# A hybrid encoder layer: zero-padded query remainders, alternating banks for the value transposes, and stores of the intra products from another queue

## The chip, the core and the metric

The kernel runs on one core of a Trainium2 chip. A core has a matrix engine (PE, which loads its stationary operand in a separate step, PEld), a vector engine (DVE), a scalar engine (ACT), GpSimd (POOL) and SyncE (SP, which here only issues DMAs). PE writes its results to PSUM, where DVE and ACT fetch them; operands lie in SBUF. The metric is the device time of one execution in microseconds (us).

## The reference

One encoder layer on 512 positions of 1024 features, in fp32:

```
x = x + 1/2 * SwiGLU_1(RMSNorm(x))
h = RMSNorm(x); p = h @ W_in
  group A: bidirectional gated delta rule, 4 heads of 128, chunks of 64:
      lmat  = strict lower part of (k*beta) k^T * decay,  tmat = (I + lmat)^-1
      intra = q k^T * decay
      scan over chunks: v_new = u - w S;  o = qg S + intra v_new;  S = S*exp(g) + kdec^T v_new
  group B: dilated softmax attention, 8 heads of 64 (queries and keys normalised, relative bias)
x = x + concat(A, B) @ W_out
x = x + 1/2 * SwiGLU_2(RMSNorm(x))
x = RMSNorm(x)
```

## The kernel before

Features lie in partitions and positions in the free dimension, 512 to a tile. An fp32 product is made of parts: a factor is split into a high part, rounded to the PE's fp32r format, and the remainder (names that end in h and l), and a projection sums three matmuls, high by high, high by low and low by high. The first feed-forward block (FFN1) runs until about 383 us, the mixer until about 760 us, the second block (FFN2) until the end.

The mixer's projections are units of a string `ORDER`: K, Q, V and Z are 128 columns each of the delta rule's keys, queries, values and gates, by head; Pa, Pb and v are the attention's queries, keys and values, by pair of heads; g0 to g3 start the grams of the four heads. PE's instruction order is fixed by hand: `interleave` merges the projections with the chain of the delta rule (grams, triangular solve, levels, scan) and with the attention, and each PE instruction is issued after the one ahead of it. The order on ACT, DVE, POOL and SP is made by a scheduler, from dependencies and from the order in which the code names them.

What the change touches:

- The weights of the mixer (`wsp`, L216) were split earlier and lie in DRAM. SP loads a half of a projection's weights at a time, 512 KB, into one of 4 buffers, so each unit needs two. A load can be issued when its buffer is free and SP has come to it.
- `gram(h)` multiplies keys by keys (`pkk`) and keys by queries (`pkq`). For both directions DVE masks `pkq` into `itr`, POOL multiplies it by the decay in `M`, and DVE writes the strict part of `pkk`, scaled, over the same `M`. Then SP stores 8 pieces of `M` to `D1` in DRAM (D in the trace) and the two `itr` to `int_d`; each of these is 128 x 4 runs of 512 bytes. The solve reads `D1` back (`MM`), the scan reads `int_d`.
- `post_val(h)` and `post_v(pr)` transpose the values of one delta-rule head and of one pair of attention heads on PE (`ptr`, `ptv`), and ACT (with DVE for `ptv`) fetches them as `vtok` and `vb`. Both took their PSUM bank from the pool `pat`, which has one bank. `pov` is another pool of one bank, in which `mix` sums the attention's outputs; `pat` also holds the transposed probabilities `pT`.
- `split_pair` prepares one pair of heads for the scores. For head i, `QA[i]` holds the high part of its queries twice, in both halves of the partitions, and `KA[i]` the high part of its keys in one half and their remainder in the other, so one matmul over 128 partitions sums two products. `ql` holds the remainders of the queries, the first head's in partitions 0 to 63 and the second's in 64 to 127.
- `score(n)`, for n from 0 to 31, makes a tile of 128 x 512 scores `pS` with two matmuls, QA by KA over 128 partitions and ql by the high half of KA over 64. DVE adds the bias and takes the maximum (L1070), ACT takes the exponential; `flip` transposes it (`pT`) and splits it (`PT`, ACT and DVE), and `mix` multiplies it by `vb`. The scores of the first half run among the scan's matmuls (`ps`), the last 16 among those of the output projection (`pd`) and of the remaining `pqk`.

Of the kernel before, what the change touches and what calls it, by code (L numbers as in the profile page):

```python
# [10 lines left out]
F32 = mybir.dt.float32  # L11
F32R = mybir.dt.float32r
# [4 lines left out]
P = 128  # L17
T = 512
NKT = 8
NF = 22  # L20
NH = 4
# [69 lines left out]
def encoder_layer(ctx, tc, xT, gu1, dn1, win, wab, wo1, wo2, gu2, dn2, cols, relb, masks, onehot, lnc, sel, out):  # L91
    nc = tc.nc
    te, ve, se, gp, sy = PEQueue(tc, nc.tensor), nc.vector, nc.scalar, nc.gpsimd, nc.sync
# [12 lines left out]
    def pfl(name):  # L106
        return ps.tile([P, T], F32, tag="fl", name=name, bufs=2)

    def pat(name):
        return ps.tile([P, T], F32, tag="at", name=name, bufs=1)  # L110
# [4 lines left out]
    def prg(name):  # L115
        return ps.tile([P, T], F32, tag="rg", name=name, bufs=2)
# [7 lines left out]
    def tmp(tag, name, n=T, dt=F32, bufs=2):  # L124
        return tp.tile([P, n], dt, tag=tag, name=name, bufs=bufs)

    def slot(tag, name=None, dt=F32):
        return xp_.tile([P, T], dt, tag=tag, name=name or tag)
# [31 lines left out]
    def lx(*a, **k):  # L160
        with tc.issue_after(act["pre"].ins):
            return se.activation(*a, **k)
# [58 lines left out]
    def sub(o, a, b):  # L221
        ve.tensor_tensor(out=o, in0=a, in1=b.bitcast(F32), op=ALU.subtract)
# [140 lines left out]
    with ExitStack() as mctx:  # L363
        mp = mctx.enter_context(tc.tile_pool(name="mp", bufs=1, reuse_waits="tile"))

        def mt(shape, name, tag=None, dt=F32, bufs=1):
            return mp.tile(shape, dt, name=name, tag=tag or name, bufs=bufs)
# [77 lines left out]
        def dhc(t):  # L445
            return t.rearrange("p (d h c) -> p d h c", d=2, h=NH)

        vb = {}

        posts = []  # L450

        def proj_v(pr):
            pt = pmm("pvb")
# [4 lines left out]
            yield ("set", f"post{len(posts) - 1}", VGV)  # L458

        def post_v(pr, u):  # L460
            ptv = pat("ptv")
            for c in range(NC):
                te.transpose(out=ptv[:, c * P:(c + 1) * P], in_=u[:, c * P:(c + 1) * P], identity=ident)
            for hh in range(2):
                t = slot(f"x{2 * pr + hh}", "vb", F32R).rearrange("p (j e) -> p j e", j=4)
                src = ptv.rearrange("p (j e) -> p j e", j=4)[:, :, hh * 64:(hh + 1) * 64]
                se.copy(t[:, :, 0:64], src)
                sub(t[:, :, 64:128], src, t[:, :, 0:64])
                vb[2 * pr + hh] = t
# [66 lines left out]
        def sc(t, d, h, c, base=0):  # L536
            i = base + d * 16 + h * 4 + c
            return t[:, i:i + 1]
# [36 lines left out]
        int_d = dr.tile([NC, P, 8, P], F32, name="int_d")  # L575
# [13 lines left out]
        def gram(h):  # L589
            hc = slice(h * 4, h * 4 + 4)  # L590
            pts = []
            for t, new in ((kT, pat), (qT, pov)):
                pt = new("ptk")
                for c in range(NC):
                    te.transpose(out=pt[:, c * P:(c + 1) * P], in_=t[:, h, c * P:(c + 1) * P], identity=ident)
                pts.append(pt)
            yield 0.86, 0.0
            for pt, w in zip(pts, (wk, wq)):
                sq = tmp("sq", "sq2")
                for c in range(NC):  # L600
                    s_ = slice(c * P, (c + 1) * P)
                    se.activation(sq[:, s_], pt[:, s_], AF.Square, accum_out=w[:, h * 4 + c:h * 4 + c + 1])
            se.copy(ktok[:, h].rearrange("p c d -> p (c d)"), pts[0])
            for w in (wk, wq):
                ve.tensor_scalar(out=w[:, hc], in0=w[:, hc], scalar1=EPS, scalar2=None, op0=ALU.add)
            ve.reciprocal(n2k[:, hc], wk[:, hc])
            gp.tensor_tensor(out=ivn[:, hc], in0=wk[:, hc], in1=hlf[:, hc], op=ALU.pow)
            ve.tensor_tensor(out=dhc(c1)[:, :, h], in0=dhc(beta)[:, :, h],
                             in1=n2k[:, hc].unsqueeze(1).broadcast_to([P, 2, NC]), op=ALU.mult)
            ve.tensor_tensor(out=dhc(bdec)[:, :, h], in0=dhc(c1)[:, :, h], in1=dhc(cs[:, 32:64])[:, :, h], op=ALU.mult)  # L610
            pkk, pkq = prg("pkk"), prg("pkq")
            for c in range(NC):
                s = slice(c * P, (c + 1) * P)
                te.matmul(pkk[:, s], lhsT=kT[:, h, s], rhs=kT[:, h, s], start=True, stop=True)
            for c in range(NC):
                s = slice(c * P, (c + 1) * P)
                te.matmul(pkq[:, s], lhsT=kT[:, h, s], rhs=qT[:, h, s], start=True, stop=True)
            yield 1.74, 0.0
            its = []
            for d in range(2):  # L620
                decv = M[d][:, h * NC:(h + 1) * NC, :]
                itr = tmp("u", "itr").rearrange("p (c i) -> p c i", c=NC)
                itv = itr if d == 0 else itr[:, ::-1, :]
                ve.tensor_tensor(out=itv, in0=pkq.rearrange("p (c i) -> p c i", c=NC),
                                 in1=INC[d].unsqueeze(1).broadcast_to([P, NC, P]), op=ALU.mult)
                gp.tensor_tensor(out=itv, in0=itv, in1=decv, op=ALU.mult)
                its.append(itr)
                for c in range(NC):
                    ve.scalar_tensor_tensor(out=decv[:, c, :], in0=pkk[:, c * P:(c + 1) * P],
                                            scalar=sc(c1, d, h, c), in1=decv[:, c, :], op0=ALU.mult, op1=ALU.mult)  # L630
            for b in range(4):
                s = slice(b * SB, (b + 1) * SB)
                for d in range(2):
                    m = slice(d * 16 + h * 4, d * 16 + h * 4 + 4)
                    sy.dma_start(out=D1[m, b, :].rearrange("m (r c) -> r m c", r=SB), in_=Mt_[s, m, s])
            for d in range(2):
                sy.dma_start(out=int_d[:, :, d * NH + h, :].rearrange("s p i -> p s i"), in_=its[d])

        pend = {}

# [43 lines left out]
            yield ("set", f"post{len(posts) - 1}", VGO)  # L684

        def post_val(h, vT):
            pt = pat("ptr")
            for c in range(NC):
                te.transpose(out=pt[:, c * P:(c + 1) * P], in_=vT[:, c * P:(c + 1) * P], identity=ident)
            for c in range(NC):  # L690
                se.mul(vtok[:, h, c, :], pt[:, c * P:(c + 1) * P], ivn[:, h * 4 + c:h * 4 + c + 1])
# [80 lines left out]
        gin = {}  # L772
# [14 lines left out]
        def split_pair():  # L787
            qn, kn = qkn[True], qkn[False]
            QA = [mt([P, T], f"QA{i}", dt=F32R) for i in range(2)]
            KA = [mt([P, T], f"KA{i}", dt=F32R) for i in range(2)]  # L790
            ql = mt([P, T], "ql", dt=F32R)
            for i in range(2):
                me = slice(64 * i, 64 * i + 64)
                ot = slice(64 - 64 * i, 128 - 64 * i)
                se.copy(QA[i][me, :], qn[me, :])
                se.copy(KA[i][me, :], kn[me, :])
                ve.tensor_copy(QA[i][ot, :], qn[me, :])
                sub(KA[i][ot, :], kn[me, :], KA[i][me, :])
                sub(ql[me, :], qn[me, :], QA[i][me, :])
            return {True: QA, False: KA, "ql": ql}  # L800

        ZTt = mt([P, 2, 16, 64], "ZT", tag="S4")
# [251 lines left out]
        def att():  # L1054
            S, PTs, ous = {}, {}, {}

            def score(n):
                pr, hh, it = n // 8, (n // 4) % 2, n % 4
                h, qk = 2 * pr + hh, S["qk"]
                me = slice(64 * hh, 64 * hh + 64)  # L1060
                ts_ = slice(it * P, (it + 1) * P)
                if it == 0:
                    S["bw"] = mt([P, 896], "bw", bufs=2)
                    vsrc = vec_d[h:h + 1, :]
                    gp.dma_start(out=S["bw"], in_=bass.AP(tensor=vsrc.tensor, offset=vsrc.offset, ap=[[1, P], [1, 896]]))
                pS = pfl("pS")
                te.matmul(pS, lhsT=qk[True][hh][:, ts_], rhs=qk[False][hh], start=True, stop=False)
                te.matmul(pS, lhsT=qk["ql"][me, ts_], rhs=qk[False][hh][me, :], start=False, stop=True)
                L = S[n] = mt([P, T], "L", bufs=2)
                ve.tensor_tensor_reduce(out=L, in0=pS, in1=S["bw"][:, 128 * it:128 * it + T], op0=ALU.add, op1=ALU.max,  # L1070
                                        scale=1.0, scalar=NEG, accum_out=mx[:, n:n + 1])
                ve.tensor_scalar(out=mx[:, 32 + n:33 + n], in0=mx[:, n:n + 1], scalar1=-1.0, scalar2=None, op0=ALU.mult)
                lx(L, L, AF.Exp, bias=mx[:, 32 + n:33 + n], accum_out=den[:, n:n + 1])
# [237 lines left out]
```

## Time and profile before

| | us |
|---|---|
| median of 3 runs | 1139.67 |
| lowest and highest | 1138.08 and 1140.06 |
| the profiled execution | 1138.61 |
| its span | 1136.5 |
| PE busy | 1085.4 (96%) |
| DVE busy | 613.7 (54%) |
| ACT busy | 440.6 (39%) |
| POOL busy | 82.7 (7%) |

The span runs from the first to the last instruction of the trace, and the execution's own time is a little longer. Times in the rows count from the start of the span. PE's clock was granted in full over nearly all of the span. A busy PE is not the same as a PE that does useful work at its full rate: a matmul's row gives its whole length through the array, and the next one starts before it ends, so the rate is read from the distance between two starts.

### The profile page before, as it was taken

The page shows a single profiled execution, that of the slowest core. Times are in us where ns is not written, and L with a number is a line of the kernel's source. Part 1 is how long each engine was busy: PE and PEld are TensorE (multiplying, and loading weights), DVE is VectorE, ACT ScalarE, POOL GpSimd, SP SyncE. Part 2 cuts the span into 40 slices and gives each one's busy share as a digit, 9 for nine tenths or more (in the row PEclk, how much of TensorE's full clock was granted, in tenths as well). Part 3 has the DMA queues.
Part 4 walks back from the last instruction along what each step waited for, and adds up shares of the span by engine and source line. Part 5 has one row for each costly group of instructions (what it writes and reads, how often), then busy time and mean ns, then how long its engine had stood idle before and what let it go on. Part 6 is the DMA issues. An engine that isn't in the chain of part 4 may idle for free.

```text
span 1136.5 us, 14357 instructions
## 1 busy us (share of the span) xinstructions
PE 1085.4 (96%) x5312; PEld 872.9 (77%) x5312; DVE 613.7 (54%) x1108; ACT 440.6 (39%) x812; POOL 82.7 (7%) x111
## 2 busy tenths in 40 slices
PE   8999999999899999989899999999999999999995
PEld 6787777777788878768678876788888888888884
DVE  5655556555444278677467778565444444532223
ACT  6534344334332227412465655434322332322221
POOL 3000000000011213320000020000000000001101
PEclk9999999999999999999899999999999999999998
DMA  7788988888983244577622353352223222333332
GB/s 258 260 280 271 295 285 284 277 287 291 306 291 105 84 135 146 186 226 241 123 92 76 118 197 120 98 199 93 93 96 109 93 93 94 97 98 102 90 96 74
DMA packets 88646, 192.00 MB, mean 169 GB/s; under 512 B 21520, under 2 KB 26416, under 8 KB 88576
## 3 DMA queue, kind: packets, MB, share of 16 engines
q1 hardware_dynamic: 85024, 180.78, 49.1%
q0 software_dynamic: 2256, 8.15, 2.2%
q10 hardware_dynamic: 1296, 2.15, 0.5%
q8 instruction: 42, 0.69, 0.2%
q14 instruction: 28, 0.23, 0.1%
HBM read 142.24 MB, written 48.81 MB: 168 GB/s over the span
## 4 chain that ended last, share of the span: by engine, by line
PE 40%; issue 13%; DVE 3%; DMA 1%; POOL 1%; ACT 0%; DVEq 0%; POOLq 0%; ACTq 0%
PE pg L53 11%; PE pd L53 11%; PE pu L53 11%; PE pd L51 3%; PE pout L53 1%; PE ps L51 1%; PE pov L51 1%; PE pS L51 1%; DMA rd_d<-dT 1%; PE pT L51 1%; PE pqk L51 1%; DMA rdb<-rd_d 0%; DVE y L1229 0%; PE pnb L51 0%; PE pr L53 0%
## 5 line engine op out<-in xcount | busy, mean ns | idle before, releaser
L176 ACT CAST whi<-wraw 128x1024 fp32r<-128x1024 f32 (+1 forms) x138 | 137.6, 998 | 266.4 <-PE pd L53 101.6
L177 DVE TENSOR_TENSOR wlo<-wraw,whi 128x1024 fp32r<-128x1024 f32 (+1 forms) x138 | 160.0, 1160 | 107.1 <-ACT whi L176 104.9
L53 PE MATMUL pg<-xh,wlo 128*128 128x512 f32 x344 | 136.1, 396 | 7.4 <-DVE wlo L177 7.3
L53 PE MATMUL pg<-xh,whi 128*128 128x512 f32 x344 | 136.8, 398 | 6.4 <-ACT whi L176 6.1
L53 PE MATMUL pu<-xh,wlo 128*128 128x512 f32 x344 | 135.4, 394 | 5.2 <-DVE wlo L177 5.1
L53 PE MATMUL pd<-hh,whi 128*128 128x512 f32 x352 | 137.4, 390 | 2.1 <-ACT whi L176 2.1
L53 PE MATMUL pd<-hh,wlo 128*128 128x512 f32 x352 | 137.5, 391 | 1.0 <-DVE wlo L177 1.0
L53 PE MATMUL pd<-hl,whi 128*128 128x512 f32 x352 | 137.1, 390 | 0.0
L53 PE MATMUL pg<-xl,whi 128*128 128x512 f32 x344 | 135.4, 394 | 0.0
L53 PE MATMUL pu<-xl,whi 128*128 128x512 f32 x344 | 134.1, 390 | 0.0
L53 PE MATMUL pu<-xh,whi 128*128 128x512 f32 x344 | 134.0, 390 | 0.0
L206 DVE TENSOR_TENSOR praw<-praw,phi 128x512 fp32r<-128x512 f32 x76 | 53.3, 706 | 117.1 <-ACT phi L205 114.2
L205 ACT CAST phi<-praw 128x512 fp32r<-128x512 f32 x76 | 47.0, 619 | 156.9 <-DMA praw<-in_win 106.3
L53 PEld LDWEIGHTS pg<-xh,wlo 128*128 128x128 f32 x344 | 65.1, 189 | 25.0 <-DVE wlo L177 11.7
L53 PEld LDWEIGHTS pg<-xh,whi 128*128 128x128 f32 x344 | 65.2, 190 | 22.5 <-ACT whi L176 8.2
L53 PEld LDWEIGHTS pu<-xh,wlo 128*128 128x128 f32 x344 | 64.6, 188 | 23.0 <-DVE wlo L177 9.9
L53 PEld LDWEIGHTS pd<-hh,whi 128*128 128x128 f32 x352 | 66.1, 188 | 16.2 <-ACT whi L176 2.6
L53 PEld LDWEIGHTS pd<-hh,wlo 128*128 128x128 f32 x352 | 66.1, 188 | 15.9 <-DVE wlo L177 2.2
L53 PEld LDWEIGHTS pd<-hl,whi 128*128 128x128 f32 x352 | 66.1, 188 | 13.7
L53 PEld LDWEIGHTS pg<-xl,whi 128*128 128x128 f32 x344 | 65.1, 189 | 14.7 <-DVE xl L269 0.9
L53 PEld LDWEIGHTS pu<-xl,whi 128*128 128x128 f32 x344 | 64.5, 188 | 13.7
L53 PEld LDWEIGHTS pu<-xh,whi 128*128 128x128 f32 x344 | 64.6, 188 | 13.0
(290 smaller groups left out, 1633.4 us busy)
## 6 DMA issues: line engine op xcount, KB each, us to landing
wraw<-in_gu SPq DMA_DIRECT2D x84, 512.0 KB, 4.2
wsp<-ws SPq DMA_DIRECT2D x76, 512.0 KB, 3.3
ws<-phi SPq DMA_DIRECT2D x76, 256.0 KB, 3.7
ws<-praw SPq DMA_DIRECT2D x76, 256.0 KB, 4.8
wraw<-in_dn SPq DMA_DIRECT2D x32, 512.0 KB, 3.5
praw<-in_win SPq DMA_DIRECT2D x56, 256.0 KB, 4.6
wraw<-in_dn SPq DMA_DIRECT2D x16, 384.0 KB, 3.5
praw<-in_wo SPq DMA_DIRECT2D x16, 256.0 KB, 3.7
```

The lines of the kernel that those rows point to most:

```text
L51: self.last = f(*a, **k)
L53: self.last = f(*a, **k)
L176: se.copy(hi[:, s], raw[:, s])
L177: ve.tensor_tensor(out=lo[:, s], in0=raw[:, s], in1=hi.bitcast(F32)[:, s], op=ALU.subtract)
L205: se.copy(hi, lo)
L206: ve.tensor_tensor(out=lo.bitcast(F32R), in0=lo, in1=hi.bitcast(F32), op=ALU.subtract)
```

## The change

It has three parts. In `split_pair` the remainder of the queries gets a tile per head, `ql[0]` and `ql[1]`, in which the other head's half is zero; the halves are set to zero once, by POOL, and the second tile shares its place with the scratch `stp` of the solve (tag "ssq"). The second matmul of a score then runs over all 128 partitions, against the whole `KA`. In `post_val` and `post_v` the bank comes from `pov` and `pat` in turn, by a counter. In `gram` POOL issues the two stores to `int_d`.

```diff
+        posts, nflip = [], [0]
+        def pflip(name):
+            nflip[0] += 1
+            return (pat, pov)[nflip[0] % 2](name)
...
         def post_v(pr, u):
-            ptv = pat("ptv")
+            ptv = pflip("ptv")
...
             for d in range(2):
-                sy.dma_start(out=int_d[:, :, d * NH + h, :].rearrange("s p i -> p s i"), in_=its[d])
+                gp.dma_start(out=int_d[:, :, d * NH + h, :].rearrange("s p i -> p s i"), in_=its[d])
...
         def post_val(h, vT):
-            pt = pat("ptr")
+            pt = pflip("ptr")
...
-            ql = mt([P, T], "ql", dt=F32R)
+            if "ql" not in gin:
+                gin["ql"] = mt([P, T], "ql", dt=F32R), tmp("ssq", "ql", dt=F32R, bufs=1)
+                for i in range(2):
+                    gp.memset(gin["ql"][i][64 - 64 * i:128 - 64 * i, :].bitcast(F32), 0.0)
+            ql = gin["ql"]
...
-                sub(ql[me, :], qn[me, :], QA[i][me, :])
+                sub(ql[i][me, :], qn[me, :], QA[i][me, :])
...
-                te.matmul(pS, lhsT=qk["ql"][me, ts_], rhs=qk[False][hh][me, :], start=False, stop=True)
+                te.matmul(pS, lhsT=qk["ql"][hh][:, ts_], rhs=qk[False][hh], start=False, stop=True)
```

The transposes run in the order V0, V1, V2, V3, v0, v1, v3, v2; so V0, V2, v0 and v3 use the bank of `pov`, and V1, V3, v1 and v2 that of `pat`. PE's own order is the same before and after.

On SP's queue, at the gram of head 0, the rows stand as follows; ws_107 and so on are the halves of the weights in the order in which they are used, D_3160 is `D1`.

```order
 L216 DMA wsp<-ws_107 128x1024
 L216 DMA wsp<-ws_108 128x1024
-L637 DMA int_d<-itr 128x4x128 x2
-L635 DMA D_3160<-M 32x4x32 x8
 L216 DMA wsp<-ws_109 128x1024
+L640 DMA D_3160<-M 32x4x32 x8
 L216 DMA wsp<-ws_110 128x1024
```

The stores to `int_d` are gone from SP, and one weight load more stands ahead of the D stores.

On the same queue, at the gram of head 3 and the start of the solve, which loads MM:

```order
 L216 DMA wsp<-ws_117 128x1024
-L637 DMA int_d<-itr 128x4x128
-L635 DMA D_3160<-M 32x4x32 x8
-L637 DMA int_d<-itr 128x4x128
 L216 DMA wsp<-ws_118 128x1024
-L811 DMA MM<-D_3160 64x1024 x2
+L640 DMA D_3160<-M 32x4x32 x8
 L216 DMA wsp<-ws_119 128x1024
+L820 DMA MM<-D_3160 64x1024 x2
```

The load of ws_118 now stands ahead of the D stores, and ws_119 between these and the loads of MM.

On ACT, around the transposes of v3 (whose result `ptv` the casts to vb fetch), before:

```order
L1086 CAST PT<-pT 128x4x128
L1105 COPY tl<-pov 64x256
L162 ACTIVATE L,den<-L,mx 128x512
L467 CAST vb<-ptv 128x4x64
L986 ACTIVATE vd<-ps,bdec 128x128 x3
L467 CAST vb<-ptv 128x4x64
L986 ACTIVATE vd<-ps,bdec 128x128
L996 ACTIVATE vn<-ps,c_3156 128x128 x4
```

And after:

```order
L1094 CAST PT<-pT 128x4x128
L162 ACTIVATE L,den<-L,mx 128x512
L1113 COPY tl<-pov 64x256
L472 CAST vb<-ptv 128x4x64 x2
L995 ACTIVATE vd<-ps,bdec 128x128 x4
L1005 ACTIVATE vn<-ps,c_3156 128x128 x4
```

The exponential of L has moved ahead of the copy of tl, and both casts to vb ahead of the four vd.

## Rows read from the trace of the kernel before

**Rows 1.** PE's waits: line and releaser, us in total, times, longest

```profile
PE pz L51 <- DMA wsp<-ws: 3.3, 1, 3.3
...
PE pc L51 <- DMA wsp<-ws: 1.7, 2, 1.3
```

**Rows 2.** Stretches: length, busy us of engines (instructions), granted clock, DMA

```profile
496.10:499.40 3.30, 2.73 (x7) 2.05 (x8) 1.36 (x3) 0.00 (x0) 0.00 (x0) 0.50 1.00 287
...
547.30:554.10 6.80, 5.59 (x15) 4.54 (x16) 5.55 (x9) 4.24 (x10) 0.00 (x0) 0.50 0.59 130
```

**Rows 3.** Timeline of SP's DMA queue: start, length, what it issues

```profile
451.00 3.81 SPq L635 DMA_DIRECT2D D<-M  x8
454.91 9.48 SPq L216 DMA_DIRECT2D wsp<-ws  x6
...
486.77 4.42 SPq L635 DMA_DIRECT2D D<-M  x8
...
491.77 0.45 SPq L216 DMA_DIRECT2D wsp<-ws  x1
```

**Rows 4.** Timeline of all engines around V3 and v0; in brackets the wait

```profile
543.59 1.14 ACT L691 ACTIVATE vtok<-ptr,ivn 128x128 f32<-128x128 f32 x4 [0.67 <-PE ptr L51]
...
544.78 0.66 PE L51 MATMUL ptr<-mk,vT 128*128 128x128 f32 x4 [1.23 <-ACT vtok L691]
...
548.51 1.11 PE L51 MATMUL ptv<-mk,vbT 128*128 128x128 f32 x4 [3.08 <-ACT vtok L691]
```

**Rows 5.** Weight loads of the second score matmul: count, busy, mean ns, idle before

```profile
L51 PEld LDWEIGHTS pS<-KA,ql 64*128 64x128 f32 x32 | 5.9, 183 | 7.7 <-issue 7.7
```

**Rows 6.** Timeline of PE where matmuls of 128 rows follow short ones

```profile
590.15 0.48 PE L51 MATMUL pvb<-xh,wsp 128*128 128x512 f32 x1
590.47 0.39 PE L51 MATMUL pvb<-xl,wsp 128*128 128x512 f32 x1
590.70 0.62 PE L51 MATMUL pvb<-xh,wsp 128*128 128x512 f32 x2
```

**Rows 7.** Timeline of all engines around one score in the third pair

```profile
716.47 0.47 PE L51 MATMUL pS<-KA,QA 128*128 128x512 f32 x1
...
716.88 0.50 PE L51 MATMUL pS<-KA,ql 64*128 64x512 f32 x1
...
717.30 0.50 PE L51 MATMUL pd<-goh,wsp 128*128 128x512 f32 x1
...
717.41 0.69 DVE L1070 CUSTOM_DVE_ANT_0 L<-pS,bw 128x512 f32<-128x512 f32 x1 [1.98 <-PE pS L51]
717.63 0.40 PE L51 MATMUL pd<-gol,wsp 128*128 128x512 f32 x1
...
718.02 0.69 DVE L222 TENSOR_TENSOR PT<-pT,PT 128x512 fp32r<-128x512 f32 x1
...
718.86 0.63 PE L51 MATMUL pT<-mk,L 128*128 128x128 f32 x4
```

**Rows 8.** Timeline of all engines around v3's transposes

```profile
607.79 0.60 PE L51 MATMUL ptv<-mk,vbT 128*128 128x128 f32 x4
608.00 0.37 ACT L1105 COPY tl<-pov 64x256 f32<-64x256 f32 x1 [2.11 <-PE pov L51]
...
608.39 0.72 ACT L162 ACTIVATE L<-L,mx 128x512 f32<-128x512 f32 x1
608.40 0.42 DVE L1106 TENSOR_TENSOR ou<-pov,tl 64x256 f32<-64x256 f32 x1 [0.52 <-ACT tl L1105]
```

**Rows 9.** Instructions on tile itr: count, ns min/median/max, first and last start

```profile
L626 POOL TENSOR_TENSOR itr<-itr,M x8: 1274/1286/1718, 448.0 to 485.5; 128x512 f32<-128x512 f32 x8
```

**Rows 10.** Instructions on tile xa, in the same columns

```profile
L1159 POOL DMA_DIRECT2D xa<-x_d x2: 756/763/770, 657.7 to 660.0; - x2
```

**Rows 11.** Timeline of all engines around POOL's store of the softmax denominators

```profile
674.00 3.20 DVE L1032 TENSOR_SCALAR otok<-otok,rs_o 128x128 f32<-128x128 f32 x16
...
674.36 2.94 POOL L1115 DMA_DIRECT2D rd_d<-dT  x1 [8.72 <-DVE dT L1114]
```

More of the change, by code (lines that the diff above doesn't have):

```diff
@@ L448, in encoder_layer @@
         vb = {}
-        posts = []
+        posts, nflip = [], [0]
+        def pflip(name):
+            nflip[0] += 1
+            return (pat, pov)[nflip[0] % 2](name)
         def proj_v(pr):
@@ L1059, in score @@
                 h, qk = 2 * pr + hh, S["qk"]
-                me = slice(64 * hh, 64 * hh + 64)
                 ts_ = slice(it * P, (it + 1) * P)
```

## The prediction, made before the changed kernel had run

> **What bounds the kernel now.** I read the list of PE's waits first, then PE's clock by stretches, and then the timelines around each wait. FFN1 fills the time up to about 383 us and FFN2 the time from 760 us; the change touches neither, so everything below happens in the mixer between. The list shows few long waits there: pz and pc on a weight DMA, 3.3 and 1.7 us [rows 1]. The timeline adds two gaps of the value transposes, 1.23 and 3.08 us [rows 4]. These five waits (pc has two) make 9.3 us, and the clock falls after the longest: to 0.50, the lower of its two levels, 1.2 instead of 2.4 GHz, for 3.3 us from 496.1 and for 6.8 us from 547.3 [rows 2]. Elsewhere in the mixer PE is busy almost without a break, so what its own instructions cost there is time as well. The span is 1136.5 us and the execution 1138.61, so 2.1 us lie around it; this execution is 1.06 below the median of 1139.67.
>
> **The score pairs.** Before, the second matmul of a score uses 64 rows of the array, and its neighbours 128. The reader is to see three intervals between starts [rows 7]: 716.47 to 716.88 is 0.41, 716.88 to 717.30 is 0.42, and the first matmul after the pair takes until 717.63, 0.33. Matmuls with 128 rows that follow short ones, as QA does, go 0.32, 0.23 [rows 6]; a further one takes 0.23 too (0.62 for two of 0.39). So the pair and its successor take 1.16 instead of 0.78. What costs is not the arithmetic: the weight load of the 64-row matmul starts late, 7.7 us over 32 loads, 0.24 each, with nothing named that it waits for [rows 5]. It is a load that is not laid under the matmul ahead of it because the shapes differ, and so is the one behind it. After, all are 128 rows: 32 x 0.38 = 12.2 us of PE time less, as an upper end. The lower end is nothing, if the lateness has another cause than the rows.
>
> Some of it is given back. PE's next transpose pT at 718.86 needs PT, for which DVE first reduces L (0.69, from 717.41) and then subtracts [rows 7]. The new second matmul starts 0.09 sooner and takes 0.39 instead of 0.50 [rows 6, 7], so this chain starts 0.20 sooner while PE comes 0.38 sooner; where the chain ends last, 0.18 is lost. I count 7 such places in the last 16 scores (1.3 us), and in the 13 scores that are mixed with the scan between 589 and 667 I take 0.4 of the gain as lost, 13 x 0.38 x 0.4 = 2.0; that share is a choice. Net 12.2 - 3.3 = 8.9, bounds 5 and 12.2.
>
> A rule speaks against this term. The Trainium skill, "TensorE: Matmul & The Clock Gate", section "Why this matters for your kernels", says that a single matmul with K=32 takes the same time as one with K=128. By that, padding buys nothing, and the sum below would be 9.6 instead of 18.5. The row disagrees: 0.42 until the next start against 0.23; but the rule speaks of one matmul and the row of a change of shape.
>
> The two added POOL memsets run once; the second waits for the solve's scratch, which shares its tile, and is long done before the scores. POOL has little else there. The four subtractions per pair keep their shapes. Cost nothing; if POOL were busy then, one memset would be about as long as its multiply, 1.3 [rows 9], once.
>
> **The value transposes.** ACT evicts V2's four transposes in 1.14 from 543.59, until 544.73; V3's have one bank with V2's and start at 544.78. v0's wait then for V3's evictions, which ACT runs between the norm's steps, until 548.51 [rows 4]. After, V2 has the ov bank, V3 the at bank, v0 the ov bank. V3 no longer waits. v0 needs V2's evictions alone, so it can start where V3 did, at 544.78 instead of 548.51: 3.73 less. Some 0.6 of waiting is left there (1.23 + 3.08 - 3.73). The clock's fall from 547.3 has then no gap ahead of it: half of the 5.59 busy us in that stretch [rows 2] comes back, 2.8. Together 6.5, bounds 3.7 (the clock falls all the same) and 7.1 (no wait left).
>
> The alternation brings a new wait at v3. Before, its transposes ran at 607.79 in the at bank. After, they want the ov bank straight behind mix's pov. ACT copies tl at 608.00 (0.37) and DVE adds ou at 608.40 (0.42), until 608.82 [rows 8], before that bank is free. The order of ACT after puts the exponential of L, 0.72 and 0.1 for its sum, ahead of tl, as the order rows show: L from about 607.9, tl 608.75, ou until 609.55. So ptv comes 1.8 late, or 1.0 if tl still were first. Behind it on PE are ps<-r,M and pqk; ACT's vb casts and then the scan's vd move with it. I take 1.8, bounds 0 and 1.8.
>
> **The stores.** SP issues eight D stores in 3.81 at 451.00, with int_d in front, and only then, at 454.91, the weights; at g3 eight D stores in 4.42 from 486.77 and one int_d, and one weight half at 491.77, for which pz waits 3.3 [rows 1, 3]. int_d waits for a POOL multiply, 1.29 by its median [rows 9], and holds all behind it on the queue. After, SP's row has one weight half ahead of g0's D stores, and one ahead of g3's. That moves the g3 half by 5 us or more; pz's wait of 3.3 and pc's two, 1.7, go: 5.0, and half of 2.73 busy us at 0.50 [rows 2], 1.4. Sum 6.4; bounds 0 (the buffer is not free sooner) and 6.4.
>
> Against it: eight issues move to POOL. Its issues for xa, also in many pieces, took 0.76 [rows 10]. One now stands between the two multiplies of each gram, so DVE's M of the second direction comes 0.76 later, and with it the D stores and the solve's input. DVE has the first direction's four products in between; in the four grams only g3's can reach PE, through the solve, which runs under the projections. Then the weight half behind g3's D stores and the two MM loads is next to be late, V2's. For both I take 1.5, between 0 and 3.3 (the wait as it was, one place later).
>
> **Sum.** 8.9 + 6.5 + 6.4 - 1.8 - 1.5 = 18.5. From 1138.61 that is 1120.1; the median stands 1.06 higher, so I say 1121.
>
> **The rivals.** (a) As summed: 1121, its own range 1116 to 1125.5, chance 0.56. (b) The scores' gain is given back to the softmax's chain on DVE and ACT: where PE comes 0.38 sooner and waits for L, the gain left is 3 of 8.9, so 1127. For it: pT at 718.86 follows the subtraction at once [rows 7]; against it: in the scan PE has other work. 0.17. (c) Padding buys nothing, as a late load has another cause than the rows: 1121 + 8.9 = 1130. Against it: no load among equal shapes is as late [rows 6]. 0.04. The rule named above speaks for this case. (d) POOL's issues are held up. One took 2.94 at 674.36, while DVE ran 16 products from 674.00, against 0.76 for xa [rows 10, 11]. At 2.2 more for each and three grams on the path: +6.6, 1127.5. Against it: other POOL issues beside a busy DVE are not so long. 0.08. The Trainium skill, "SBUF — State Buffer", section "SBUF: two separate sides", has a rule of this kind: some DVE operations lock POOL out while it writes a DMA's descriptors. The row at 674.36 is consistent with it but names no cause. (e) All of the scores' gain is kept and no weight wait stays: 12.2 + 6.5 + 6.4 - 1.8 = 23.3, or 1116.4 and, with v0's 0.6 gone as well, 1115.8. 0.08. (f) Slower: PE's work gets shorter than the chains it waits for, and the clock falls there. Such an event costs, by the pair of gaps at V3 and v0, 4.3 of wait and 2.8 of clock, 7.1. It takes 2.6 of these in the 150 us of the scores to eat 18.5, and three (21.3) to come out slower by more than 0.2%. For it: the low stretches follow waits of 3 us [rows 1, 2]; against: the scores' waits are far shorter. 0.05, of which 0.04 is slower than before. (g) It comes to no change because the weights' buffer, not SP, set their time, and the clock dips elsewhere: 1139, 0.02.
>
> **The numbers.** 0.2% is 2.3 us, about what a measurement of this kernel can tell from no change. Cases (a) to (e) are faster by more than that, 0.93; same 0.03; slower 0.04. The likeliest is 1121. Cases (b), (c) and (d) reach to 1130, and the sum with all upper gains and no costs (12.2 + 7.1 + 6.4 = 25.7) to 1114; I set 1113 and 1130; that range leaves out (f), (g) and the edges of the others.
>
> **What would show it.** Intervals of 0.32 and 0.23 in the score pair, with the second weight load's 7.7 us of idle time gone. No wait of V3's ptr, less than 1 us for v0's, and some 1 to 2 us before v3's ptv, with tl and ou as its cause. No weight wait at Q3, V1 and Z3; the clock at 1.00 from 499 to 554. POOL's stores at 0.76 each. It is wrong if pS still has a late weight load, if the waits of pT grow by more than 5 us in sum, if the clock falls anywhere between 560 and 760 other than at 687, or if a weight wait of over 3 us shows at V2.

## The result, and the profile after

The changed kernel takes 1126.28 us, the median of 4 runs between 1121.98 and 1131.03; the kernel before took 1139.87 in the runs beside it (1138.08 to 1143.75). The ratio is 0.9874, with a 95% interval from 0.9852 to 0.9896: 13.6 us less by the medians. Forecast were 1121 and 18.5 us less, with a range from 1113 to 1130. The profiled execution took 1124.95, its span 1123.2.

PE's order is the same before and after, so the start of each PE instruction can be set beside its start before. The mixer falls into three stretches: A from the first pkq to the first pvb (grams, weights), B from there to the first pS (the value transposes of V2, V3 and v0), C from the first pS to the last one.

| | before | after | difference |
|---|---|---|---|
| first pkq starts | 445.42 | 446.18 | |
| A, to the first pvb | 66.75 | 62.84 | -3.91 |
| B, to the first pS | 48.92 | 42.56 | -6.36 |
| C, to the last pS | 168.49 | 164.66 | -3.84 |
| last pS to the end of the span | 406.96 | 406.94 | 0.0 |

So 14.1 us less in the mixer; 0.76 more ahead of it, in a part that the change doesn't touch, leaves 13.3 in the span. B came as forecast (6.5). A gave 3.91 where the sum had 6.4 - 1.5 = 4.9. C gave 3.84 where the sum had 8.9 - 1.8 = 7.1. The time ahead of the first pkq lies between 444.1 and 449.2 in the profiles below, though no edit touches it; A, B and C leave out this scatter, which the whole time contains.

First the list of PE's waits in the changed kernel (us in total, times, longest). Rows of FFN1 and FFN2 are left out.

```profile
PE pT L51 <- ACT L L162: 2.5, 1, 2.5
PE pkq L51 <- DVE M L634: 1.7, 1, 1.7
PE pT L51 <- DVE PT L222: 1.6, 2, 0.9
...
PE ptv L51 <- DVE ou L1114: 1.4, 1, 1.4
PE pz L51 <- DVE qk L652: 1.3, 1, 1.3
...
PE ps L51 <- DVE st L997: 1.2, 1, 1.2
...
PE ptv L51 <- ACT vtok L696: 0.8, 1, 0.8
PE pc L51 <- DMA wsp<-ws: 0.6, 2, 0.3
```

The weight waits of 3.3 and 1.7 [rows 1] have shrunk to 0.6, and the transposes' wait for vtok from 3.08 [rows 4] to 0.8. In their place stand new ones, all behind DVE or ACT: pkq for M, pz for qk, ptv for ou, ps for st, and pT's, of which one alone is 2.5.

The weight loads of the second score matmul (count, busy, mean ns, idle before), and the timeline of PE around a score of the third pair:

```profile
L51 PEld LDWEIGHTS pS<-KA,ql 128*128 128x128 f32 x32 | 6.1, 192 | 0.0
```

```profile
703.47 0.48 PE L51 MATMUL pS<-KA,QA 128*128 128x512 f32 x1
703.79 0.39 PE L51 MATMUL pS<-KA,ql 128*128 128x512 f32 x1
704.02 0.39 PE L51 MATMUL pd<-goh,wsp 128*128 128x512 f32 x1
704.25 0.39 PE L51 MATMUL pd<-gol,wsp 128*128 128x512 f32 x1
```

The load's idle time of 7.7 us [rows 5] is gone, and the intervals are 0.32, 0.23 and 0.23 instead of 0.41, 0.42 and 0.33 [rows 7]. For this score the forecast holds to the hundredth. Over C and the two intervals behind it, the intervals next to a pS are 11.56 us shorter in sum, against 12.2 forecast; those that end in a wait are 7.4 longer, and the rest differ by under 0.1. The question of the experiments is where these 7.4 come from.

The timeline at v0 and, below, at v3:

```profile
540.44 1.66 ACT L696 ACTIVATE vtok<-ptr,ivn 128x128 f32<-128x128 f32 x6 [0.67 <-PE ptr L51]
...
541.63 0.66 PE L51 MATMUL ptv<-mk,vbT 128*128 128x128 f32 x4 [0.80 <-ACT vtok L696]
```

```profile
595.35 0.72 ACT L162 ACTIVATE L<-L,mx 128x512 f32<-128x512 f32 x1 [1.34 <-DVE mx L1080]
...
596.19 0.37 ACT L1113 COPY tl<-pov 64x256 f32<-64x256 f32 x1
596.60 0.42 DVE L1114 TENSOR_TENSOR ou<-pov,tl 64x256 f32<-64x256 f32 x1 [0.74 <-ACT tl L1113]
...
597.07 0.66 PE L51 MATMUL ptv<-mk,vbT 128*128 128x128 f32 x4 [1.38 <-DVE ou L1114]
```

v0's ptv waits 0.80 for V2's evictions, 0.6 were forecast. At v3 ACT runs the exponential of L ahead of tl, as its order had shown; DVE adds ou after that, and ptv waits 1.38 (1.5 later than before, relative to the pov ahead of it; 1.8 forecast). Of the prediction's signs of being wrong none came: the waits of pT grew by 3.2 in sum and not by over 5, the weight wait at V2 is 0.3, and the clock falls in C only behind the same pT as before (687.3 then, 675.1 now).

### The profile page after: what moved, and what is told of

The parts are those of the page before. It is cut to its first block, busy times and chain, and to the rows that moved or that the text cites. A ratio compares the mean times of both kernels' runs of the same rounds, so it can differ in the third digit from the quotient of the medians.

```text
span 1123.2 us, 14359 instructions
## 1 busy us (share of the span) xinstructions
PE 1071.6 (95%) x5312; PEld 871.1 (78%) x5312; DVE 613.1 (55%) x1108; ACT 441.1 (39%) x812; POOL 90.3 (8%) x121
```

## The experiments

Differences of A, B and C below are to the kernel before, from the starts of the same PE instructions in each profile. A fall of the clock to 0.50 for 3.4 us in C is worth 1.5 to 1.7 there: before has one (from 687.3), after (from 675.1) and pad_only too, the other kernels none, but for best_rows64 (below). Small differences in A and B of the kernels with one part come from pz's weight wait, 3.9 in pad_only and 4.0 in flip_only instead of 3.3, and from the low clock in B, 3.4 us long in pad_only and pool_only instead of 6.8.

| kernel | A | B | C | median, us | ratio to before, 95% |
|---|---|---|---|---|---|
| changed kernel | -3.91 | -6.36 | -3.84 | 1126.28 | 0.9874 (0.9852 to 0.9896) |
| pad_only | +1.30 | -1.11 | -5.97 | 1133.33 | 0.9946 (0.9928 to 0.9965) |
| flip_only | +0.94 | -6.34 | +0.02 | 1135.37 | 0.9964 (0.9940 to 0.9987) |
| pool_only | -3.82 | -1.00 | -1.10 | 1133.99 | 0.9951 (0.9931 to 0.9970) |
| ob_behind_L | -3.93 | -6.35 | -8.26 | 1123.40 | 0.9854 (0.9814 to 0.9895) |
| v3_in_at | -3.93 | -6.36 | -7.88 | 1122.78 | 0.9845 (0.9803 to 0.9886) |
| stores_behind | -6.16 | -6.36 | -6.61 | 1125.16 | 0.9862 (0.9830 to 0.9894) |
| all_three | -5.07 | -6.36 | -10.05 | 1118.46 | 0.9805 (0.9777 to 0.9833) |
| denominators_sp | -3.45 | -6.34 | -9.97 | 1119.88 | 0.9829 (0.9804 to 0.9854) |
| all_three_sp | -5.71 | -6.35 | -11.93 | 1113.99 | 0.9786 (0.9751 to 0.9821) |
| best_rows64 | -5.82 | -6.34 | -1.94 | 1123.67 | 0.9865 (0.9844 to 0.9885) |

**Each part alone.** pad_only takes the lines of the diff on `ql`, flip_only those on `pflip`, pool_only this one:

```diff
-                sy.dma_start(out=int_d[:, :, d * NH + h, :].rearrange("s p i -> p s i"), in_=its[d])
+                gp.dma_start(out=int_d[:, :, d * NH + h, :].rearrange("s p i -> p s i"), in_=its[d])
```

> Only the zero-padded ql, the rest as before. The prediction's term: 8.9 us less than before (gross 12.2, 3.3 given back by the softmax and scan chains). The rival read from the changed kernel's trace: the pairs give about 11.6 less between starts, but waits of PE behind the chains take back 5 or more of it, so 4 to 6.5 less than before; the waits of ps on DVE st and of pT on ACT L grow, as DVE stands behind ob, which waits for the denominators' DMA. If a lone matmul of 64 rows cost no more than one of 128: no change.

> Only the alternation of banks for the value transposes. The prediction: 6.5 less at V3 and v0 (3.7 of wait, 2.8 of clock) and 1.8 more at v3, so 4.7 less than before. The rival: the fall of the clock comes at another place, then 1.9 less.

> Only the stores to int_d issued by POOL. The prediction: the three weight waits (5.0) and 1.4 of clock go, 1.5 of new waits come, so 4.9 less than before. The rival read from the changed kernel's trace: waits of pkq on DVE M (1.7 instead of 0.7) and of pz on DVE qk (1.3) take back more, so 3.5 to 4 less. If POOL's stores were held up by DVE: no gain or slower.

Each acts in its own stretch: pool_only in A, flip_only in B, pad_only in C, and the medians (5.7, 3.6 and 5.0 less) add up to 14.3, near the 13.6 of all. pad_only's pairs are 11.58 shorter, as in the changed kernel, and its waits 5.38 longer, so the padding itself is worth 6 and the rival's size, not 8.9. The 7.4 of the changed kernel is this, v3's 1.54 and 0.5 more at two pT (0.38 and 0.16). flip_only's C hides v3's cost (1.07) and a wait of ps (0.23) behind the clock that doesn't fall there. pool_only shows that the whole of A comes from the stores: the weight waits of 5.08 in sum are gone, and 1.67 before pkq, 1.30 before pz and 0.63 before a pc have come.

**Is it 64 rows, or the change of rows?** The kernel before, with the second score matmul issued twice (its product counts twice):

```diff
-                te.matmul(pS, lhsT=qk["ql"][me, ts_], rhs=qk[False][hh][me, :], start=False, stop=True)
+                te.matmul(pS, lhsT=qk["ql"][me, ts_], rhs=qk[False][hh][me, :], start=False, stop=False)
+                te.matmul(pS, lhsT=qk["ql"][me, ts_], rhs=qk[False][hh][me, :], start=False, stop=True)
```

> The kernel before, with the second score matmul of 64 rows issued twice in a row, so that its product is added twice. If the change of shape between neighbours makes the weight load late: the second of the two starts 0.23 after the first, its load lies under the first, and the matmul after the pair still starts 0.42 later. If 64 rows are slow by themselves: 0.42 between the two as well. If rows never matter to a lone matmul: 0.23 everywhere, which the kernel before already contradicts.

In the kernel before, two weight loads start late, that of the 64 rows and the one behind it:

```profile
716.87 0.18 PEld L51 LDWEIGHTS pS<-KA,ql 64*128 64x128 f32 x1 [0.24 <-issue]
...
717.30 0.19 PEld L51 LDWEIGHTS pd<-goh,wsp 128*128 128x128 f32 x1 [0.24 <-issue]
```

In ql_twice, the loads of ql, and PE around one score (x2 are the two of 64 rows):

```profile
L51 PEld LDWEIGHTS pS<-KA,ql 64*128 64x128 f32 x64 | 9.5, 187 | 8.0 <-issue 8.0
```

```profile
728.49 0.48 PE L51 MATMUL pS<-KA,QA 128*128 128x512 f32 x1
...
728.89 0.29 PEld L51 LDWEIGHTS pS<-KA,ql 64*128 64x128 f32 x2 [0.24 <-issue]
728.89 0.73 PE L51 MATMUL pS<-KA,ql 64*128 64x512 f32 x2
...
729.55 0.19 PEld L51 LDWEIGHTS pd<-goh,wsp 128*128 128x128 f32 x1 [0.36 <-issue]
729.55 0.50 PE L51 MATMUL pd<-goh,wsp 128*128 128x512 f32 x1
...
729.88 0.39 PE L51 MATMUL pd<-gol,wsp 128*128 128x512 f32 x1
```

The idle time is 8.0 us over 64 loads, as it was 7.7 over 32: only the first of each two is late, and again the load behind the second. From the first of the two to the next pd are 0.66, where one alone took 0.42: the second adds 0.24, which is what a matmul of 128 rows takes among its like. Its one run took 1152.72, with 32 more matmuls, and is not compared. (The medians of the 32 split the 0.66 into 0.34 and 0.32, not into the 0.23 and 0.42 that were expected.) So a matmul of 64 rows adds no more than one of 128 rows, 0.24 against 0.23; the change of rows on either side of it costs. The Trainium skill, "TensorE: Matmul & The Clock Gate", section "Why this matters for your kernels", says that one matmul with K=32 takes as long as one with K=128. The trace agrees for 64 rows by what the second one adds, and shows what a change of rows costs.

**What holds the scores.** The largest wait in C is pT's of 2.48 at 673.79. All engines ahead of it in the changed kernel:

```profile
661.72 3.20 DVE L1041 TENSOR_SCALAR otok<-otok,rs_o 128x128 f32<-128x128 f32 x16
...
662.08 2.94 POOL L1123 DMA_DIRECT2D rd_d<-dT  x1 [8.34 <-DVE dT L1122]
...
666.70 1.08 POOL L1127 DMA_DIRECT2D rdb<-rd_d  x2 [1.68 <-issue]
...
670.53 0.69 DVE L1130 TENSOR_TENSOR ob<-ou,rdb 128x512 f32<-128x512 f32 x1 [2.53 <-DMA rdb<-rd_d]
...
671.14 0.68 DVE L1078 CUSTOM_DVE_ANT_0 L<-pS,bw 128x512 f32<-128x512 f32 x1
...
672.92 0.72 ACT L162 ACTIVATE L<-L,mx 128x512 f32<-128x512 f32 x1 [0.43 <-DVE mx L1080]
...
673.79 0.66 PE L51 MATMUL pT<-mk,L 128*128 128x128 f32 x4 [2.48 <-ACT L L162]
```

To be read from below: pT waits for the exponential of L, this for the reduction of L on DVE at 671.14, and DVE had stood 2.53 in front of ob, for rdb. That is the reciprocal denominators of the pair just closed, on their way through DRAM: POOL stores them (rd_d) and loads them back (rdb). The store's issue took 2.94, from 662.08 to 665.02; DVE's 16 products of otok end at 664.92. The row had this length before too [rows 11], and ob waited then as well, but PE came later. Behind pT the clock fell (length, busy us of the engines, granted clock):

```profile
675.10:678.30 3.20, 3.20 (x12) 2.79 (x11) 1.74 (x5) 1.82 (x6) 0.00 (x0) 0.50 0.00 0
```

Two more waits of this kind stand in C: 1.18 before ps, with DVE idle for 1.92 ahead of ob, and 0.88 before pT at 712.26, with 0.92. ob_behind_L takes the reduction of L out of this: ob stands behind the next one.

```diff
-                ve.tensor_tensor(out=ob[:, ::-1], in0=ous[pr], in1=rdb, op=ALU.mult)
-                obs.append(ob)
+                return pr, rdb
+            def close2(pr, rdb):
+                ob = slot(f"x{2 * pr}", "ob")
+                with tc.issue_after(act["red"].ins):
+                    ve.tensor_tensor(out=ob[:, ::-1], in0=ous[pr], in1=rdb, op=ALU.mult)
+                obs.append(ob)
...
-                ve.tensor_tensor_reduce(out=L, in0=pS, in1=S["bw"][:, 128 * it:128 * it + T], op0=ALU.add, op1=ALU.max,
+                act["red"] = ve.tensor_tensor_reduce(out=L, in0=pS, in1=S["bw"][:, 128 * it:128 * it + T], op0=ALU.add, op1=ALU.max,
```

`close2` is called for each of the first three pairs (the expectation names two) after the score that lies two further on.

> The changed kernel with ob, the multiplication by the reciprocal denominators, placed behind the next reduction of L on DVE in the first two pairs; PE's order is the same. If the score gain is given back because DVE stands behind ob, which waits for a DMA round trip: the waits of 1.2 (ps) and 2.5 (pT) in the changed kernel fall below 0.6 each, and the low clock after the second goes, so 3 to 5 less than the changed kernel, some 17 to 18 less than before. If the chain from pS over L and the exponential to pT is too long by itself: the waits stay within 0.5, and the time is that of the changed kernel, 13 to 14 less than before.

```profile
664.38 0.67 DVE L1078 CUSTOM_DVE_ANT_0 L<-pS,bw 128x512 f32<-128x512 f32 x1
...
667.05 0.69 DVE L1134 TENSOR_TENSOR ob<-ou,rdb 128x512 f32<-128x512 f32 x1 [1.99 <-DMA rdb<-rd_d]
...
669.49 0.63 PE L51 MATMUL pT<-mk,L 128*128 128x128 f32 x4 [1.71 <-DVE mx L1080]
```

The wait before ps is 0.00 instead of 1.18. L's reduction at 664.38 no longer stands behind ob, but DVE waits there all the same, 1.99, and holds the next small operation (mx) back, so pT still waits 1.71. C is 4.4 shorter than in the changed kernel, 1.6 of it the clock. The theory holds for the first pair. For the second, the wait fell by 0.77 and not by the 1.9 expected; in v3_in_at and stores_behind, which leave ob in its place, it is 2.23 and 1.97, so a good part of the 0.77 can be scatter of the round trip. The third pair's 0.88 fell to 0.24, but in these two kernels it fell to 0.21 and 0.01. The median (1123.40) is 2.9 below the changed kernel's, with intervals that overlap.

So the round trip itself was made shorter, in the changed kernel, with ob at its old place in the second pair:

```diff
-                gp.dma_start(out=rd_d[2 * pr:2 * pr + 2, :].rearrange("h (i t) -> (h i) t", i=4), in_=dT)
+                sy.dma_start(out=rd_d[2 * pr:2 * pr + 2, :].rearrange("h (i t) -> (h i) t", i=4), in_=dT)
...
-                    gp.dma_start(out=rdb[64 * hh:64 * hh + 64, :],
+                    sy.dma_start(out=rdb[64 * hh:64 * hh + 64, :],
```

> The changed kernel with the store and the loads of the denominators issued by SP instead of POOL, and nothing else. If the issue of 2.9 on POOL beside DVE is what makes DVE stand at ob in the second pair: its wait falls from 2.5 to about 0.5, and the pT wait of 2.5 below 1; some 2 to 3 less than the changed kernel by the end of the scores. If ob's place on DVE is what counts: the waits stay above 1, and the gain is under 1.

```profile
660.90 3.21 DVE L1041 TENSOR_SCALAR otok<-otok,rs_o 128x128 f32<-128x128 f32 x16
...
661.00 0.28 SPq L1123 DMA_DIRECT2D rd_d<-dT  x1
...
667.10 0.67 DVE L1130 TENSOR_TENSOR ob<-ou,rdb 128x512 f32<-128x512 f32 x1
...
670.34 0.66 PE L51 MATMUL pT<-mk,L 128*128 128x128 f32 x4
```

SP issues the store in 0.28 beside the same 3.21 of otok, ob waits for nothing, and pT's wait is gone (a row with a wait has brackets). In the first pair the wait before ps is gone too, but there DVE's order moved ob behind st and qk, so that pair shows nothing of the issue alone. C is 6.1 shorter than in the changed kernel (1.5 of it clock), the whole 1119.88. The Trainium skill, "SBUF — State Buffer", section "SBUF: two separate sides", says that DVE in some of its modes locks POOL out while POOL writes the descriptors of a DMA, and that SP and ACT don't have this; the trace agrees: 2.94 on POOL, ending 0.10 after DVE's products, against 0.28 on SP. It doesn't show which mode DVE was in. That the products hold the store, and not POOL by itself, can be read from ql_twice, where the same store comes just behind them and takes 0.53:

```profile
683.47 3.23 DVE L1032 TENSOR_SCALAR otok<-otok,rs_o 128x128 f32<-128x128 f32 x16
...
687.17 0.53 POOL L1116 DMA_DIRECT2D rd_d<-dT  x1 [12.01 <-DVE dT L1115]
```

**The two waits that the change brought.** v3_in_at is the changed kernel with `pflip("ptv") if pr < 2 else pat("ptv")`.

> The changed kernel, with the transposes of v3 back in the at bank. If v3's wait of 1.4 on DVE ou comes from the ov bank alone: it is gone, 1.4 to 1.6 less than the changed kernel in the mixer, with no wait put in its place. If the scan behind it is the limit there, the wait comes back within 3 us as a wait of ps: 0 to 0.5 less.

```profile
598.06 0.60 PE L51 MATMUL ptv<-mk,vbT 128*128 128x128 f32 x4
```

v3's ptv follows pov without a wait; 1.54 come back, and nothing takes its place (the next waits are the same to 0.1, until pT's of 2.23). The rest of C's difference to the changed kernel, 2.5, is the clock (1.5) and shorter pT waits at 674 and 712 (0.9).

In stores_behind both stores come behind the second multiplication on POOL. First the changed kernel at the gram in which pkq waits for 1.70:

```profile
467.28 1.29 POOL L631 TENSOR_TENSOR itr<-itr,M 128x512 f32<-128x512 f32 x1 [0.59 <-DVE itr L629]
...
468.87 0.81 POOL L642 DMA_DIRECT2D int_d<-itr  x1 [0.29 <-POOL itr L631]
...
469.65 1.90 DVE L430 SCALAR_TENSOR_TENSOR qT<-xp,col,qT 128x512 f32<-128x512 f32 x1
469.71 1.28 POOL L631 TENSOR_TENSOR itr<-itr,M 128x512 f32<-128x512 f32 x1
...
471.48 1.11 DVE L634 SCALAR_TENSOR_TENSOR M<-pkk,c,M 128x128 f32<-128x128 f32 x4
...
472.64 0.60 PE L51 MATMUL pkq<-qT,kT 128*128 128x128 f32 x3 [1.70 <-DVE M L634]
```

A wait of 0.29 and the issue, 0.81, stand between the multiplications, so the second comes 1.1 late. DVE meanwhile does a step of qT, which takes 1.90 beside this multiplication (0.73 without one, at 472.51), and M of the second direction ends 1.6 later than before, counted from the first M; pkq waits for it. pz's wait is behind POOL too: at the gram of head 3, M waits for the second multiplication, and qk comes right behind M.

```profile
489.60 1.13 DVE L634 SCALAR_TENSOR_TENSOR M<-pkk,c,M 128x128 f32<-128x128 f32 x4 [1.32 <-POOL itr L631]
...
490.81 0.63 DVE L652 TENSOR_TENSOR qk<-pqk,R 128x512 f32<-128x512 f32 x1
```

```diff
-                gp.tensor_tensor(out=itv, in0=itv, in1=decv, op=ALU.mult)
+                mul = gp.tensor_tensor(out=itv, in0=itv, in1=decv, op=ALU.mult)
...
-                gp.dma_start(out=int_d[:, :, d * NH + h, :].rearrange("s p i -> p s i"), in_=its[d])
+                with tc.issue_after(mul.ins):
+                    gp.dma_start(out=int_d[:, :, d * NH + h, :].rearrange("s p i -> p s i"), in_=its[d])
```

> The changed kernel, with both stores to int_d issued by POOL behind the second multiplication of a gram. If the waits of pkq on DVE M (1.7) and of pz on DVE qk (1.3) come from the 1.1 us that a store puts between POOL's two multiplications: pkq waits about 0.6 and pz about 0.2, so 2.2 less than the changed kernel by the start of V2. If they come from SP's D stores or from DVE's own order: both waits stay.

```profile
467.06 2.54 POOL L631 TENSOR_TENSOR itr<-itr,M 128x512 f32<-128x512 f32 x2 [0.58 <-DVE itr L629]
469.54 1.57 POOL L643 DMA_DIRECT2D int_d<-itr  x2
...
489.42 0.69 DVE L653 TENSOR_TENSOR qk<-pqk,R 128x512 f32<-128x512 f32 x1 [1.18 <-DMA int_d<-itr]
```

The multiplications follow each other; pkq waits 0.06 there and 0.62 at the next gram (0.70 before, 0.00 in the changed kernel), pz 0.94 instead of 1.34. A is 2.25 shorter, the size expected, but not by the parts expected: pkq's two waits give 0.85, pz's 0.4, and 0.9 is two waits of pc for weights, which come and go in other kernels too (in ob_behind_L the first is gone and the second 0.62). pz has another wait in place of the old one: qk now stands 1.18 for the landing of a store to int_d, since `itr` and `qk` take turns in the same two buffers (tag "u"). all_three, all_three_sp and best_rows64 have the same edit; there qk stands 1.5 to 1.6, and pz waits as long as in the changed kernel (1.3 to 1.4).

**Together.** all_three is the changed kernel with these three edits (v3 in at, stores behind, ob behind L), all_three_sp has the denominators on SP as well, best_rows64 is that without the padding. (all_three without the padding, all_three_64, gave no result.)

> The changed kernel with v3 in the at bank, both stores behind the second multiplication, and ob behind the next reduction of L. If the three act apart: 1.5 + 2.2 + 2.6 = 6.3 less than the changed kernel, and 20 less than before. If the score pairs' gain is limited by the chains anyway, what is gained at v3 and at the grams is lost again in the pT waits: 3 to 4 less than the changed kernel.

> all_three with the store and the two loads of the denominators issued by SP instead of POOL. If POOL's issue of 2.9 us beside DVE's multiplications of otok is what makes the second pair's round trip long: ob then waits under 0.5 for rdb instead of 2, the pT wait of 1.6 falls to 0.5 or less, 1 to 1.5 less than all_three. If the round trip is long by the transfers themselves, or SP's queue stands behind weight loads: ob waits as long, and weights come later, 0 to 2 more.

> all_three_sp with the padding undone: one ql tile, second score matmul over 64 rows. If the padding's gain in pad_only (6.1 in the mixer from the first score on) was held down by chains that all_three_sp relieves: 11.6 gross less some 3.3 of small waits, so this kernel takes 8 us more than all_three_sp from the first score to the end. If the padding is worth what it was in pad_only: 6 more.

all_three takes 1118.46, 7.8 less than the changed kernel. In the trace A and C are 7.4 shorter, 1.6 of it the clock, so the three edits give 5.8 of the 6.3 expected: in sum they act nearly apart, though A gives only 1.16 of stores_behind's 2.25 (pz waits 1.3 again, and a pc 0.5 for weights), and 0.7 comes from the third pair's pT. all_three_sp takes 1113.99, 2.1% less than the kernel before; pT's wait of 1.60 falls to 0.09. It is 4.5 less than all_three by the medians, of which A and C show 2.5. best_rows64 then asks what the padding is worth here: C is 10.0 longer without it. best_rows64 has a low stretch from 549.5 that all_three_sp has not, worth 1.6; without it 8.4 are left, against 6.0 in pad_only. The pairs are 12.0 longer, and the waits 3.1 shorter.

## Why the prediction was right, and which of its terms were off

The time lies within the stated range, but 0.8 above the 1116 to 1125.5 of case (a), the likeliest; it is nearest to the 1127 of rival (b), which took the scores' gain too low (3, where pad_only has 6.0) and the stores' too high, so that its nearness is luck. By the trace, 4.4 us are missing from the 18.5: 3.3 in C, 1.0 in A and 0.1 in B.

- **Score pairs: right in mechanism, too large by 3.** The gross term was right (12.2 forecast, 11.6 measured). The small losses where PE comes sooner than its chain were right in sum, 3.3 forecast and 3.1 measured in all_three_sp against best_rows64, partly by luck: those among the scan were 1.0 and not 2.0, those behind it 2.1 and not 1.3. The step that failed is the net of 8.9, against 6.0 in pad_only: it counted chains that start sooner with the scores, and none of fixed length. The denominators' round trip has one, DVE waits for it in order, and behind it stands the reduction of L. That is 2.3 of the 5.4 that pad_only gives back (5.4 - 3.1), in the waits behind the first three ob: ob_behind_L takes the first away, denominators_sp the second. The rows were there before: an ob with a wait for rdb, and the 2.94 of rows 11, which the prediction used only to price POOL's issues in another place (rival d). Rival (b) had the place, the chain of the softmax, and was too hard with 3 of 8.9.
- **Value transposes at V3 and v0: right.** 6.5 forecast, 6.36 measured, 6.34 alone.
- **v3: right.** 1.8 forecast, 1.54 measured, read from ACT's order; v3_in_at shows that it was the bank.
- **Stores: right, too large by 1.** The three weight waits went, for 6.4 with the clock. What came in their place was mis-sized: 2.5 instead of 1.5, and at another place. It was expected as a late weight half at V2 (0.3 came) and was pkq's and pz's wait behind POOL. The 0.76 between the two multiplications had been seen, and it was assumed that only g3's could reach PE; it is 1.1 with the wait ahead of it, and M of g1's second direction, which ends 1.6 later, is what the pkq of g2 waits for. stores_behind shows the cause for pkq; for pz it is read from the changed kernel's rows, since moving the stores put another wait in that place.
- **Rival (d)** did not come: the eight stores took 0.8 each. **(c)** is refuted by pad_only, **(f)** by the waits of C, which are longer but whose sum stays below the gain. **(e)** needed the whole of the scores' gain, **(g)** none in A; neither came.

What stays open: the clock's falls in C. Of the kernels in the table, before, after and pad_only have one behind the second pair's pT, best_rows64 one at its first scores, the others none, and that shifts a comparison of two kernels by 1.5 to 1.7. Each trace is one execution: the mean granted clock of the changed kernel's four runs is 0.990 in the profiled one and 0.992 to 0.994 in the others, so the clock doesn't fall equally often in every execution of a kernel.

## What to carry to other kernels

A gain on the bound engine is paid out only as far as nothing of fixed length stands in the queues behind it: look for a DMA round trip that an in-order engine waits for, and price it before the gain. A matmul of fewer rows among those of 128 cost through its own weight load and the next one, so padding it with zeros, where the operands allow it, is worth a trial (32 of them gave 6.0 us net here, and 8.4 with the round trip shortened). Moving a DMA's issue to an idle engine moves a wait into that engine's other work: put it behind the work that others wait for, and look at who needs the buffer that the store reads.

## What the runs showed of the hardware that was not expected

- The second of two matmuls of 64 rows starts 0.34 after the first, though its load isn't late, and the one behind it comes sooner for it.
- A store of 4 KB (8 x 128 fp32) took POOL 2.94 us to issue beside DVE's 16 products of otok, in all of the nine kernels in which the two met, ending 0.10 after the last product; 0.53 behind the products in ql_twice, 0.52 at the other pairs, and 0.28 on SP.
- A step of qT on DVE took 1.90 where a multiplication on POOL ran beside 1.28 of it, and 0.73 without one. In the kernel before, where a multiplication ran beside 0.53 of a step, the step took 0.74 and the multiplication 1.72 instead of 1.29.
- Whether the clock falls after a wait doesn't go by the wait's length alone: it fell after pT's 1.42 before, 2.09 in pad_only and 2.48 after, and not after 2.23 in v3_in_at or 1.97 in stores_behind; in best_rows64 it fell at 549.5 with no wait of PE over 0.1 in the 10 us ahead of it.
